# Half A's first layer norm: its transposes move from the GLA's PSUM bank to the three banks of the dense products

## The chip, the cores and the metric

One core of one Trainium2 chip runs one program. The metric is the device time of one execution in microseconds (us), the median of several runs; lower is better. Before the change it is 3109.51 us, the median of three runs that lie between 3102.37 and 3113.97 us.

## The reference

The program is one inference step of a two-layer streaming encoder on 1024 prompt frames of a new stream and 64 frames of a running stream, all in float32, width 1024. Layer 0 projects its input and feeds two token mixers, RWKV-7 (eight heads of 64, a matrix state that is carried from chunk to chunk) and GLA (chunked linear attention, four heads, state 64 by 128, also carried). Their outputs are joined and go through an output projection. Layer 1 has softmax attention over the frame's own chunk of 64 and the eight chunks before it. In each layer the mixer's result is added to the scaled input and normalised, then a SwiGLU of hidden width 2816 follows, with a second norm:

```
x = layer_norm(DEEPNORM_ALPHA * x + mix, ln1_w, ln1_b)
x = layer_norm(DEEPNORM_ALPHA * x + swiglu(x, ffn_w_in, ffn_w_out), ln2_w, ln2_b)
layer_norm(x) = (x - mean) * rsqrt(var + 1e-5) * w + b
```

The outputs are the frames after layer 1, the mixers' states and the attention's keys and values.

## The kernel before, in words

**Halves.** The 1088 frames lie in two halves. Half A has 448 columns: 384 prompt frames and the 64 frames of the running stream, so four token tiles of 128, 128, 128 and 64. Half B has the other 640 prompt frames. Half B's mixers need half A's states, but half A's dense work does not need half B's mixers, so the two are put beside each other.

**Products.** Every dense product is made in three passes with operands split into a high and a low part (`hi`, `lo`): high times high, high times low, low times high. `gemm_ws` (L116) holds 128 weight columns and streams the half's activations, all columns of a half at once; `gemm_ts` (L128) holds a tile of tokens and streams 512 weight columns. The 64 frames of the running stream have a packed form: their high and low parts lie side by side and two passes do, after which VectorE adds both halves of the result (L827 and L829).

**PSUM.** There are eight banks at this stage. Three, tag `g` of the pool `gp`, are handed out by `bank()` (L140) and take every dense product. Five belong to the mixers (`sbank`, L403): tags `a` (one bank), `b` (one), `c` (two) for RWKV-7 and `d` (one) for GLA, where the GLA's scores and transposed keys (`gpa`), outputs and state updates (`gps`) and transposed output (`gpy`) take turns. `sbank` gives the `d` bank to any name that is not in its table:

```
STAGE = {"pa": "a", "pb": "a", "pt": "a", "pz": "b", "ps": "c", "py": "c", "pss": "c", "gpa": "d", "gps": "d", "gpy": "d"}
tag = self.STAGE.get(name, "d")
self.tpsum = lambda: self.sbank("tps")
```

`tpsum` is what the layer norm (L899), the cache set-up (L1132) and the key part of `qk` (L1173) call for a bank to transpose into. So with the third line, which `run` sets at L1350, the layer norm's transposes use the GLA's one bank.

**The place.** `run` starts half B's mixers as two generators, `r` (RWKV-7, 24 steps) and `g` (GLA, 20 steps, one chunk of one head pair each), writes four steps of each (`self.PRE`), then half A's output projection with its layer norm (L1399), then the remaining steps of both, then half A's SwiGLU (`ffn`, L1405). In `proj` (L856) the second group of weights has the layer norm as its `after`: in `tsg` (L841 to L846) each token tile gets its two products of 512 columns, each added to the accumulator by VectorE, and then `tile(i)` of the layer norm.

**One tile of the layer norm** (L877 to L909): two `bn_stats` (L884) and an aggregate (L886) on VectorE, the reciprocal root on GpSimd (L888, L889), then for each half of 512 columns, j = 0 and 1, the scaling (VectorE L892; for j = 0 then ScalarE L894 and GpSimd L895, for j = 1 VectorE L897). Then `tpsum()` gives a bank, TensorE transposes four blocks of 128 columns into it (L902), and `split` (L111) empties it: ScalarE writes the high part into `xh` (L113) and VectorE the low part into `xl` (L114). After that the bank can be given to another tile. Four token tiles with two halves make eight such uses of a bank.

The SwiGLU's first product streams all 448 columns, so its passes over the column blocks 0 to 3 wait for j = 0 of all four tiles, and those over 4 to 7 for j = 1.

**The order of the work.** A planner orders the instructions of each engine when the program is built (`schedule_with_timeline_sim=True`, L1611). It goes by its own model of times, prefers what was written earlier in the program, and gives a tile its PSUM bank when the first instruction that writes it is put in the order. On the chip each engine then keeps that order, and an instruction that waits holds up all that stand behind it on its engine. VectorE, ScalarE and GpSimd are shared by the layer norm, the products' evacuation, the splitting of weights (L101, L106, L108) and the mixers.

Of the kernel before, what the change touches and what calls it, by code (L numbers as in the profile page):

```python
# [83 lines left out]
class Kern:  # L84
# [1255 lines left out]
    def run(self):  # L1340
# [55 lines left out]
        for _ in range(self.PRE):  # L1396
            next(r)
            next(g)
        self.proj(0, acc0, "w_om", self.layer_norm(0, acc0, "ln1", 0), pa)  # L1399
        for _ in r:  # L1400
            next(g, None)
        for _ in g:
# [212 lines left out]
```

## Time and profile before

| | us |
|---|---|
| median of three runs | 3109.51 |
| their lowest and highest | 3102.37, 3113.97 |
| the profiled execution's own time | 3102.95 |
| its span, first to last instruction | 3101.2 |
| TensorE busy in the span | 3007.5 |
| VectorE busy | 2016.0 |
| GpSimd busy | 1366.7 |
| ScalarE busy | 1270.8 |

PE is TensorE's matmul, PEld its weight load, DVE VectorE, ACT ScalarE, POOL GpSimd, SPq the queue that issues the transfers. A timeline's row gives the start and the duration in us, the engine, the line of the kernel, the operation, the tiles as output<-inputs, shapes and the number of instructions; in brackets stands the idle time before it and who ended it. A row of the table by stretches gives for each engine its busy time and number of instructions, then the clock that TensorE was granted (1.00 is full), the transfers' share and rate. Matmuls overlap, so the durations of neighbours add up to more than the time between their starts. Between 606.9 and 641 us after the span's start there is no dense product but the first of the SwiGLU; I call this stretch the gap.

### The profile page before, as it was taken

The page shows a single profiled execution, that of the slowest core. Times are in us where ns is not written, and L with a number is a line of the kernel's source. Part 1 is how long each engine was busy: PE and PEld are TensorE (multiplying, and loading weights), DVE is VectorE, ACT ScalarE, POOL GpSimd, SP SyncE. Part 2 cuts the span into 40 slices and gives each one's busy share as a digit, 9 for nine tenths or more (in the row PEclk, how much of TensorE's full clock was granted, in tenths as well). Part 3 has the DMA queues.
Part 4 walks back from the last instruction along what each step waited for, and adds up shares of the span by engine and source line. Part 5 has one row for each costly group of instructions (what it writes and reads, how often), then busy time and mean ns, then how long its engine had stood idle before and what let it go on. Part 6 is the DMA issues. An engine that isn't in the chain of part 4 may idle for free.

```text
span 3101.2 us, 50069 instructions
## 1 busy us (share of the span) xinstructions
PE 3007.5 (97%) x17468; PEld 2676.5 (86%) x17468; DVE 2016.0 (65%) x4941; ACT 1270.8 (41%) x2761; POOL 1366.7 (44%) x1489
## 2 busy tenths in 40 slices
PE   8999999899999999999999999999999999899998
PEld 7888888688888888798999898898899988899987
DVE  5677875879898764455554466245566668866667
ACT  4454554344454334243443132355444434333322
POOL 2354534444454334343342233244445546654444
PEclk9999999889999999999999999999899999999999
DMA  6553334533533228343342222866454443322212
GB/s 195 148 161 115 109 110 124 146 104 106 151 105 106 91 97 294 118 153 120 113 134 98 82 95 101 247 200 175 121 153 135 117 175 122 122 86 80 98 68 75
DMA packets 298492, 399.29 MB, mean 129 GB/s; under 512 B 125504, under 2 KB 218552, under 8 KB 298240
## 3 DMA queue, kind: packets, MB, share of 16 engines
q1 hardware_dynamic: 297088, 393.48, 41.2%
q8 instruction: 138, 2.26, 0.3%
q10 hardware_dynamic: 1152, 2.62, 0.2%
q14 instruction: 114, 0.93, 0.1%
HBM read 323.63 MB, written 75.51 MB: 129 GB/s over the span
## 4 chain that ended last, share of the span: by engine, by line
PE 77%; DVE 8%; DMA 7%; POOL 2%; issue 2%; ACT 2%; SPq 1%; POOLq 0%; ACTq 0%; DVEq 0%
PE gps L124 11%; PE gps L126 11%; PE gps L125 11%; PE gps L135 7%; PE gps L136 7%; PE gps L138 7%; PE gps L1065 3%; PE gps L1066 3%; PE gps L1067 3%; PE op L1328 2%; PE tp L1302 2%; DVE t L549 1%; DVE x L551 1%; PE sps L1286 1%; PE sps L1287 1%
## 5 line engine op out<-in xcount | busy, mean ns | idle before, releaser
L108 POOL TENSOR_TENSOR wl<-wr,wh 128x512 fp32r<-128x512 f32 (+2 forms) x297 | 521.7, 1760 | 669.3 <-ACT wh L101 612.0
L124 PE MATMUL gps<-xh,wh 128*128 128x320 f32 (+1 forms) x2188 | 747.7, 342 | 12.5 <-ACT xh L215 6.0
L125 PE MATMUL gps<-xl,wh 128*128 128x320 f32 (+1 forms) x2188 | 746.5, 341 | 0.6 <-DVE xl L216 0.6
L126 PE MATMUL gps<-xh,wl 128*128 128x320 f32 (+1 forms) x2188 | 745.9, 341 | 0.3 <-DVE wl L106 0.2
L101 ACT CAST wh<-wr 128x1024 fp32r<-128x1024 f32 x360 | 375.6, 1048 | 465.9 <-PE gps L125 135.6
L106 DVE TENSOR_TENSOR wl<-wr,wh 128x512 fp32r<-128x512 f32 (+2 forms) x297 | 293.8, 990 | 242.2 <-ACT wh L101 239.8
L124 PEld LDWEIGHTS gps<-xh,wh 128*128 128x128 f32 x2188 | 415.6, 190 | 34.4 <-ACT xh L215 6.0
L126 PEld LDWEIGHTS gps<-xh,wl 128*128 128x128 f32 x2188 | 415.6, 190 | 18.6 <-issue 0.8
L125 PEld LDWEIGHTS gps<-xl,wh 128*128 128x128 f32 x2188 | 415.5, 190 | 18.3 <-DVE xl L216 1.0
L1297 POOL TENSOR_SCALAR s<-s,mx 128x640 f32<-128x640 f32 (+5 forms) x144 | 205.3, 1426 | 258.7 <-DVE mx L1296 236.3
L138 PE MATMUL gps<-wh,xl 128*128 128x512 f32 x661 | 258.9, 397 | 5.4 <-DVE xl L216 4.8
L135 PE MATMUL gps<-wh,xh 128*128 128x512 f32 x661 | 259.9, 399 | 3.9 <-DVE acc L829 1.9
L136 PE MATMUL gps<-wl,xh 128*128 128x512 f32 x661 | 261.5, 397 | 0.0
L135 PE MATMUL gps<-wh,hh 128*128 128x512 f32 x572 | 224.8, 396 | 1.6 <-ACT wh L101 1.3
L136 PE MATMUL gps<-wl,hh 128*128 128x512 f32 x572 | 225.5, 396 | 0.0
L827 DVE TENSOR_TENSOR acc<-acc,gps 128x512 f32<-128x512 f32 x216 | 143.6, 680 | 89.6 <-PE gps L138 82.3
L138 PE MATMUL gps<-wh,hl 128*128 128x512 f32 x484 | 189.6, 397 | 1.6 <-DVE hl L943 1.6
L549 DVE TENSOR_TENSOR t<-lt,x 16x48 f32<-16x48 f32 (+9 forms) x540 | 149.3, 276 | 36.0 <-DMA lt<-l_d 25.5
L1295 ACT ACTIVATE s<-s,mx 128x640 f32<-128x640 f32 (+5 forms) x144 | 96.4, 669 | 149.6 <-DVE mx L1294 145.2
L138 PEld LDWEIGHTS gps<-wh,xl 128*128 128x128 f32 x661 | 124.9, 189 | 33.8 <-DVE xl L216 5.4
L135 PEld LDWEIGHTS gps<-wh,xh 128*128 128x128 f32 x661 | 125.0, 190 | 32.8 <-issue 2.5
L136 PEld LDWEIGHTS gps<-wl,xh 128*128 128x128 f32 x661 | 125.2, 189 | 28.0 <-DVE wl L106 1.1
(406 smaller groups left out, 6312.0 us busy)
## 6 DMA issues: line engine op xcount, KB each, us to landing
wr<-in_w_fi SPq DMA_DIRECT2D x176, 512.0 KB
wr<-in_w_fo SPq DMA_DIRECT2D x88, 512.0 KB
wr<-in_w_in SPq DMA_DIRECT2D x44, 512.0 KB
wr<-in_w_qk SPq DMA_DIRECT2D x32, 512.0 KB
wr<-in_w_o SPq DMA_DIRECT2D x24, 512.0 KB
qs<-qd SPq DMA_DIRECT2D x32, 320.0 KB
wr<-in_w_om SPq DMA_DIRECT2D x16, 512.0 KB
wr<-in_w_v SPq DMA_DIRECT2D x16, 512.0 KB
```

Of the source, the lines that this page charges most:

```text
L101: self.A.copy(hi, raw)
L106: self.V.tensor_tensor(lo[:, :h], raw[:, :h], hi[:, :h].bitcast(F32), op=ALU.subtract)
L108: self.G.tensor_tensor(lo[:, h:], raw[:, h:], hi[:, h:].bitcast(F32), op=ALU.subtract)
L124: self.T.matmul(ps, hi[:, kt, :], xh, start=(kt == 0), stop=False)
L125: self.T.matmul(ps, hi[:, kt, :], xl, start=False, stop=False)
L126: self.T.matmul(ps, lo[:, kt, :], xh, start=False, stop=(kt == nk - 1))
L135: self.T.matmul(ps, xh, wh, start=(i == 0), stop=False)
L136: self.T.matmul(ps, xh, wl, start=False, stop=(lo is None and i == n - 1))
L138: self.T.matmul(ps, cols(lo(kt)), wh, start=False, stop=(i == n - 1))
L549: V.tensor_tensor(tv, lt[:, j, w:16].unsqueeze(2).to_broadcast([m, r, w]), x[:, 0, j, 0:w].unsqueeze(1).to_broadcast([m, r, w]), op=ALU.mult)
L827: self.V.tensor_tensor(a, a, ps[:m], op=ALU.add)
L1297: G.tensor_scalar(s[:m, :nk], s[:m, :nk], mx[:m, 3:4], None, op0=ALU.mult)
```

## The change

Around half A's output projection in layer 0, `tpsum` is set to `bank` and set back afterwards:

```
-        self.proj(0, acc0, "w_om", self.layer_norm(0, acc0, "ln1", 0), pa)
+        self.tpsum = self.bank
+        self.proj(0, acc0, "w_om", self.layer_norm(0, acc0, "ln1", 0), pa)
+        self.tpsum = lambda: self.sbank("tps")
```

The eight tiles of transposes of this one layer norm are then taken from the three `g` banks, which they share with the products, and no longer from the `d` bank, which is left to the GLA. `bank()` counts its calls and, once a second pool of banks exists (from L1493 on), picks the pool by the count modulo 8. The change adds eight calls, so the choice at every later call is the same. No instruction is added or taken out: 32 transposes, eight ScalarE casts and eight VectorE subtractions get another address. What uses `tpsum` later (the cache set-up beside the SwiGLU, half A's second norm and the rest) is as before. Since a bank is a resource of the planner, the order of all engines is planned anew from there on.

## The prediction

> **What bounds the kernel now.** I read the page's head first, then the table by stretches, then TensorE's and VectorE's timelines across the gap.
>
> ```profile
> span 3101.2 us, 50069 instructions
> ```
>
> ```profile
> 482.00:606.90 124.90, 110.19 (x670) 95.45 (x670) 82.00 (x235) 49.79 (x139) 51.92 (x80) 0.93 0.51 137
> 606.90:641.00 34.10, 28.16 (x136) 22.25 (x135) 29.78 (x77) 15.57 (x45) 22.86 (x30) 0.54 0.33 117
> 641.00:1152.00 511.00, 508.45 (x3076) 436.43 (x3076) 414.08 (x1268) 218.77 (x614) 223.64 (x341) 0.99 0.36 108
> 1152.00:1360.00 208.00, 199.33 (x944) 169.03 (x943) 107.49 (x163) 74.41 (x104) 90.14 (x67) 0.98 0.60 199
> 1900.00:2200.00 300.00, 286.95 (x1706) 262.49 (x1706) 147.03 (x339) 134.45 (x264) 126.07 (x108) 0.97 0.64 191
> 2600.00:3101.00 501.00, 476.45 (x2732) 439.94 (x2730) 348.44 (x470) 172.77 (x245) 267.74 (x213) 0.98 0.26 91
> ```
>
> TensorE sets the time nearly everywhere: of the 511 us of half A's SwiGLU it is idle 2.55. The gap, 606.9 to 641, is the exception that the change touches: the granted clock is 0.54, VectorE works 29.78 of 34.10 us, and the SwiGLU waits for the layer norm. So the change can win two things: a shorter gap, and GLA work moved from the SwiGLU's stretch, where each us of TensorE counts, into the gap.
>
> Seven of the eight uses of the layer norm's one bank on TensorE (L902), with two instructions near its end, and on VectorE what empties the bank (L114) and what comes before it; the rows between are left out:
>
> ```profile
> 599.40 0.60 PE L902 MATMUL tps<-ident,acc 128*128 128x128 f32 x4
> 605.50 0.63 PE L902 MATMUL tps<-ident,acc 128*128 128x128 f32 x4
> 616.79 1.11 PE L902 MATMUL tps<-ident,acc 128*128 128x128 f32 x4
> 621.22 1.08 PE L902 MATMUL tps<-ident,acc 128*128 128x128 f32 x4 [0.44 <-DVE xl L114]
> 625.26 1.09 PE L902 MATMUL tps<-ident,acc 128*128 128x128 f32 x4 [0.65 <-DVE xl L114]
> 633.50 0.69 PE L902 MATMUL tps<-ident,acc 64*128 64x64 f32 x4
> 636.14 0.37 PE L618 MATMUL ps<-uv,tok 128*64 128x64 f32 x1
> 639.98 0.69 PE L902 MATMUL tps<-ident,acc 64*128 64x64 f32 x4
> 640.59 0.74 PE L125 MATMUL gps<-xl,wh 128*128 128x448 f32 x1
> ```
>
> ```profile
> 602.25 0.74 DVE L897 SCALAR_TENSOR_TENSOR acc<-acc,rstd,gb 128x512 f32<-128x512 f32 x1
> 604.68 0.67 DVE L114 TENSOR_TENSOR xl<-tps,xh 128x512 fp32r<-128x512 f32 x1
> 607.69 2.31 DVE L549 TENSOR_TENSOR t<-lt,x 16x28 f32<-16x28 f32 x1
> 613.62 0.66 DVE L827 TENSOR_TENSOR acc<-acc,gps 64x512 f32<-64x512 f32 x1
> 614.21 0.67 DVE L114 TENSOR_TENSOR xl<-tps,xh 128x512 fp32r<-128x512 f32 x1
> 617.53 0.69 DVE L829 TENSOR_TENSOR acc<-acc,gps 64x512 f32<-64x512 f32 x1
> 620.39 0.68 DVE L114 TENSOR_TENSOR xl<-tps,xh 128x512 fp32r<-128x512 f32 x1
> 624.42 0.69 DVE L114 TENSOR_TENSOR xl<-tps,xh 128x512 fp32r<-128x512 f32 x1
> 629.91 0.74 DVE L897 SCALAR_TENSOR_TENSOR acc<-acc,rstd,gb 64x512 f32<-64x512 f32 x1 [0.33 <-POOL rstd L889]
> 635.33 0.41 DVE L114 TENSOR_TENSOR xl<-tps,xh 128x256 fp32r<-128x256 f32 x1
> 641.16 0.39 DVE L114 TENSOR_TENSOR xl<-tps,xh 128x256 fp32r<-128x256 f32 x1
> ```
>
> Three of the seven handovers are tight: the split ends at 605.35, 621.07 and 625.11, and the next transposes start 0.15 us later. Tile 1's second half was scaled by 602.99 and was transposed only at 621.22. The last tile's second half was scaled at 630.65, its bank was empty at 635.74, and its transposes came at 639.98, behind RWKV-7 work that the planner had put there.
>
> **The change, part by part.** No instruction comes or goes, so the instructions themselves cost nothing. Three things can move the time.
>
> *First, the last handover.* With a bank of its own the last half can follow the other one: the transposes at 633.50 end where the next instruction starts, about 634.1, and 0.6 us more brings the second set to 634.7. Then the SwiGLU's L125 hangs on the split at 635.33, which ends at 635.74, and could start at about 635.8 where it starts at 640.59: 4.8 us earlier. What ran in the meantime, 636.14 to 639.98 (3.84 us, at a clock of 0.54), has to be done later, at full clock, for about half, 1.9 us. The net is -2.9 us.
>
> *Second, the handovers before it.* Tiles 1 and 2 can be transposed and split as soon as they are scaled. The splits cost VectorE the same 0.67 us each, whenever they come. What can be won is that no layer norm work is left waiting when the last tile's sums arrive. The trace has a stage without a shared bank: half A's second norm, whose eight uses go round other mixer banks.
>
> ```profile
> 1165.44 0.69 DVE L829 TENSOR_TENSOR acc<-acc,gps 64x512 f32<-64x512 f32 x1
> ...
> 1176.36 0.41 DVE L114 TENSOR_TENSOR xl<-ps,xh 128x256 fp32r<-128x256 f32 x1
> ```
>
> From the last sum to the end of the last split it takes 11.3 us (1165.44 to 1176.77); in the gap it takes 24.0 (617.53 to 641.55). The difference, 12.7 us, is the most that the first two parts can win together. In these 12.7 us TensorE is busy for 28.16/34.10 of the time, 10.5 us, at half clock, so some 5.2 us return later: -7.5 net. The other end is zero, if VectorE's order and not the bank sets the gap. I take -5.0, between -2.9 and -7.5, because three tight handovers say that the bank counts beyond the last one, and because VectorE, 87% busy, keeps the rest.
>
> *Third, the GLA.* Its rows on TensorE around the gap, with the product that follows each piece, and two groups of its instructions in the SwiGLU's stretch:
>
> ```profile
> 591.88 0.28 PE L756 MATMUL gpy<-ident,gon 128*128 128x128 f32 x1
> 647.38 0.33 PE L725 MATMUL gpa<-gqk,gbqk 128*128 128x64 f32 x2
> 647.58 0.45 PE L125 MATMUL gps<-xl,wh 128*128 128x448 f32 x1
> 652.23 0.38 PE L738 MATMUL gps<-gv,gba 128*128 128x128 f32 x2
> 652.82 0.45 PE L124 MATMUL gps<-xh,wh 128*128 128x448 f32 x1
> ```
>
> ```profile
> L409 DVE TENSOR_TENSOR gbqk<-gqk,bdk 128x256 f32<-128x256 f32 x15 | 6.8, 456 | 0.3 <-PE gps L739 0.2
> L742 POOL TENSOR_SCALAR gse<-gS,geb 128x128 f32<-128x128 f32 x15 | 12.1, 805 | 12.8 <-DVE gS L744 10.6 <-DVE x L551 2.1
> ```
>
> It has no TensorE work from 591.88 to 647.38, when the layer norm leaves the bank. Its next step can go on in the gap now. Its steps follow each other at some 20 us (this one and the next start at 647.38 and 666.07), so one or two fit there. Between the starts, a step costs the SwiGLU's stretch 0.2 us for the scores (647.38 to 647.58), 0.59 for the outputs (652.23 to 652.82) and about 0.1 for the last transpose: 0.9. Two steps save 1.8 us there. On VectorE a step has six instructions, the longest 456 ns, so at most 2.7 us; two steps put up to 5.4 us in front of, or between, the layer norm's, where VectorE is the busiest engine. The planner prefers what is written earlier, which is the layer norm, so most of it should fall into waits. The ends are -1.8 and +3.6; I take 0.
>
> What the GLA brings along on GpSimd can also slow VectorE, as a weight split does in the gap now:
>
> ```profile
> 606.41 3.55 POOL L108 TENSOR_TENSOR wl<-wr,wh 128x1024 fp32r<-128x1024 f32 x1 [2.28 <-ACT wh L101]
> ```
>
> Beside it L549, at 607.69, takes 2.31 us for 28 elements. The Trainium skill (SBUF — State Buffer, section "Who interferes with whom") says that a VectorE instruction with two inputs in SBUF contends with a GpSimd instruction that reads SBUF, and that the one issued first holds the shared port; this trace agrees (2.31 us). By this rule a GLA step's scaling of the state (L742, 805 ns) could hold VectorE once a step, 1.6 us for two, and the sum would be 3106.1 where it is 3104.5 without.
>
> **The sum.** 3102.95 (the profiled execution's own time, span 3101.2 and 1.75 around it) less 5.0 is 3097.95. That execution lies 6.56 us below the median of the runs, so against the median I predict 3109.5 - 5.0 = **3104.5 us**. About 0.5%, 15.5 us, is what a measurement of this kernel can tell from no change; my forecast lies within it.
>
> **The rivals.**
>
> *The bank was not the limit.* VectorE sets the gap; splits come no earlier because VectorE's order is the same. For it: 29.78 of 34.10 us busy, and TensorE's waits for the bank add up to only 1.09 us (0.44 and 0.65). Against it: the last handover, where VectorE had nothing to do with the 4.2 us. Time: 3109.5.
>
> *The products' banks run short: slower.* The last tile's two packed products and the tiles 0 and 1 of the layer norm, written before them and so preferred, want the same three banks. If tiles 0 and 1 hold all three, the last packed product starts late. Its eight matmuls end at 606.6 now, and its sum is taken at 613.62.
>
> ```profile
> 606.19 0.39 PE L136 MATMUL gps<-wl,xpk 128*128 128x512 f32 x1
> ```
>
> Nothing is lost as long as it ends by 613.6. If its bank comes only with the split at 614.21, which ends at 614.88, eight matmuls of 0.4 at half clock bring it to 618, and the last tile is 4.4 us late: 3113.9. It decides once a layer norm half holds a product's bank past about 611 with the other two taken as well. Against it: two banks come free at 604.75 and 605.35 in the order of now.
>
> *The new plan is luckier or worse elsewhere.* The plan is made anew from here on, with a model that isn't the chip. From 1152 on TensorE's idle time is 8.67 + 13.05 + 24.55 = 46.3 us in three stretches (length less busy). A third to a half of it is 15 to 23 us: 3081 to 3089 where it is saved on top of the gain of 5, 3120 to 3133 where it is added, with and without that gain. For it: nothing in this trace shows how much a plan moves. Against it: the stretches with idle time begin with transfers and norms that stay as they are.
>
> *The tight end.* Everything goes as in the second norm and two GLA steps fit in: -7.5 - 1.8 = -9.3, so 3100.
>
> *The change doesn't do what it says.* If the planner still puts the last half's transposes behind RWKV-7's work at 639.98, the bank is there and unused. The time is that of the first rival.
>
> **How the numbers follow.** My forecast, 3100 to 3108: 0.38. The bank was not the limit, or the plan leaves it unused: 0.18. Banks run short: 0.12. The tight end: 0.10. A new plan that is luckier by a third to a half of the idle time: 0.13; worse: 0.09. Faster by over 0.5% (below 3094) is the luckier plan, and 0.03 of the tight end with a little of the same luck: 0.16. Slower by over 0.5% (above 3125) is two thirds of the worse plan, 0.06, and 0.04 of the short banks with some of it: 0.10. Within: 0.74. The range reaches into both plans, from 3085 to 3123; the runs before alone spread over 11.6 us.
>
> **What the changed profile would show.** L902 writes `gps` tiles in the gap. Right: the last half's transposes follow the other half's within 1 us, the distance from the last sum (L829) to the last split (L114) falls from 24.0 to between 11 and 19 us, and the gap is about 5 us shorter; `gpa` and `gpy` appear between 592 and 641, and in the SwiGLU's stretch TensorE still idles below 5 us. The first rival: L829 to L114 stays near 24. Short banks: TensorE waits before L135 or L136 on `xpk`, and the sum at 613.62 comes later than about 618. A new plan: the gap changes as I say, but the stretches after 1152 differ from the rows above by more than 5 us. I am wrong if the gap grows, or if the total moves by more than 15 us while the gap does not.

## The result, and the profile after

The changed kernel is slower: 3122.01 us, the median of five runs between 3116.84 and 3126.81, against 3105.07 us for the kernel before on the same chip. The ratio is 1.0052, with a 95% interval of [1.0038, 1.0065]: 16 us lost, where the prediction had 5 won. All ratios below are to the kernel before in the same comparison. Its medians lay between 3101.6 and 3105.1 in these, all below the 3109.51 that were given at first.

The profiled span grew by 19.0 us, from 3101.2. TensorE's timeline across the gap, the rows where one kind of work gives way to the next; the columns are those of the prediction's timelines:

```profile
span 3120.2 us, 50083 instructions
```

```profile
600.52 1.09 PE L902 MATMUL gps<-ident,acc 128*128 128x128 f32 x8
601.38 0.48 PE L135 MATMUL gps<-wh,xh 128*128 128x512 f32 x1
...
608.06 0.39 PE L138 MATMUL gps<-wh,xl 128*128 128x512 f32 x1
609.49 0.43 PE L725 MATMUL gpa<-gqk,gbqk 128*128 128x64 f32 x2 [0.54 <-DVE gy L758]
615.84 1.97 PE L902 MATMUL gps<-ident,acc 128*128 128x128 f32 x8 [2.13 <-POOL acc L895]
617.46 0.77 PE L135 MATMUL gps<-wh,xh 128*128 128x512 f32 x1
...
624.64 0.39 PE L138 MATMUL gps<-wh,xl 128*128 128x512 f32 x1
635.24 1.97 PE L902 MATMUL gps<-ident,acc 128*128 128x128 f32 x8
636.86 0.78 PE L135 MATMUL gps<-wh,xpk 128*128 128x512 f32 x1
...
641.61 0.39 PE L136 MATMUL gps<-wl,xpk 128*128 128x512 f32 x1
643.91 0.39 PE L725 MATMUL gpa<-gqk,gbqk 128*128 128x64 f32 x2
656.81 1.19 PE L902 MATMUL gps<-ident,acc 64*128 64x64 f32 x8
661.00 0.74 PE L125 MATMUL gps<-xl,wh 128*128 128x448 f32 x1
1171.82 0.60 PE L902 MATMUL pz<-ident,acc 128*128 128x128 f32 x4
```

Read down the line numbers: eight transposes, a tile's products, eight transposes, the next tile's products, and so on. Products and transposes of the layer norm strictly alternate. Before, the last product began at 606.19, with two of the eight sets of transposes done, and the other six followed. Now tile 1's products begin 0.86 us after tile 0's transposes begin, tile 2's 1.62 us after tile 1's, and the packed ones of tile 3 1.62 us after tile 2's. From the end of its products each tile needs 7.4, 10.2 and 14.8 us until its own transposes (608.45 to 615.84, 625.03 to 635.24, 642.00 to 656.81). These stretches used to overlap with other tiles' products; now they stand in a row.

The kernel before starts its second norm here:

```profile
1152.16 0.60 PE L902 MATMUL pz<-ident,acc 128*128 128x128 f32 x4
```

The SwiGLU's first L125 comes at 661.00, 20.4 us later than before. From there to the second norm's first transposes it is 510.82 us (before 511.57, from 640.59 to 1152.16), and the rest of the span takes 1948.4 (before 1949.0). So the whole loss arises in the gap. The table by stretches, for two stretches of the length of the SwiGLU's, the second row of the kernel before:

```profile
659.90:1171.80 511.90, 506.46 (x3009) 431.85 (x3009) 399.62 (x1211) 209.41 (x578) 207.53 (x318) 0.99 0.36 106
```

```profile
640.60:1152.20 511.60, 509.05 (x3078) 436.94 (x3078) 414.68 (x1270) 219.27 (x614) 223.86 (x342) 0.99 0.36 108
```

TensorE has 2.6 us less to do there, since GLA steps have moved ahead of it (L725 at 609.49, 625.34 and 643.91), but it idles 5.4 us instead of 2.6. What GLA gave was not kept.

### The profile page after: what moved, and what is told of

The parts are those of the page before. It is cut to its first block, busy times and chain, and to the rows that moved or that the text cites. A ratio compares the mean times of both kernels' runs of the same rounds, so it can differ in the third digit from the quotient of the medians.

```text
span 3120.2 us, 50083 instructions
## 1 busy us (share of the span) xinstructions
PE 3009.3 (96%) x17468; PEld 2673.5 (86%) x17468; DVE 2019.6 (65%) x4941; ACT 1269.2 (41%) x2761; POOL 1352.7 (43%) x1489
## 4 chain that ended last, share of the span: by engine, by line
PE 78%; DVE 8%; DMA 7%; POOL 2%; issue 2%; ACT 2%; SPq 1%; POOLq 0%; ACTq 0%; DVEq 0%
PE gps L124 11%; PE gps L125 11%; PE gps L126 11%; PE gps L135 8%; PE gps L136 8%; PE gps L138 7%; PE gps L1065 3%; PE gps L1067 3%; PE gps L1066 3%; PE op L1328 2%; PE tp L1302 2%; DVE t L549 1%; DMA wr<-in_w_in 1%; PE sps L1286 1%; DVE x L551 1%
## 5 line engine op out<-in xcount | busy, mean ns | idle before, releaser
L125 PE MATMUL gps<-xl,wh 128*128 128x320 f32 (+1 forms) x2188 | 744.5, 340 | 0.6 <-DVE xl L216 0.6
L125 PEld LDWEIGHTS gps<-xl,wh 128*128 128x128 f32 x2188 | 413.9, 189 | 18.8 <-DVE xl L216 1.0
L138 PE MATMUL gps<-wh,xl 128*128 128x512 f32 x661 | 259.4, 398 | 5.4 <-DVE xl L216 4.8
L135 PE MATMUL gps<-wh,xh 128*128 128x512 f32 x661 | 260.7, 400 | 4.0 <-DVE acc L829 1.9
L136 PE MATMUL gps<-wl,xh 128*128 128x512 f32 x661 | 261.7, 397 | 0.0
L135 PE MATMUL gps<-wh,hh 128*128 128x512 f32 x572 | 225.5, 398 | 1.3 <-ACT wh L101 1.0
L136 PE MATMUL gps<-wl,hh 128*128 128x512 f32 x572 | 226.3, 398 | 0.0
L827 DVE TENSOR_TENSOR acc<-acc,gps 128x512 f32<-128x512 f32 x216 | 143.5, 679 | 95.5 <-PE gps L138 88.5
L138 PE MATMUL gps<-wh,hl 128*128 128x512 f32 x484 | 189.1, 396 | 0.0
L549 DVE TENSOR_TENSOR t<-lt,x 16x48 f32<-16x48 f32 (+9 forms) x540 | 140.2, 260 | 42.4 <-DMA lt<-l_d 32.2
L551 DVE TENSOR_TENSOR x<-x,t 16x48 f32<-16x48 f32 (+9 forms) x540 | 153.9, 285 | 10.4
L138 PEld LDWEIGHTS gps<-wh,xl 128*128 128x128 f32 x661 | 125.1, 189 | 33.7 <-DVE xl L216 5.3
L135 PEld LDWEIGHTS gps<-wh,xh 128*128 128x128 f32 x661 | 125.3, 190 | 32.7 <-issue 2.3
```

The lines of the kernel that those rows point to most:

```text
L125: self.T.matmul(ps, hi[:, kt, :], xl, start=False, stop=False)
L135: self.T.matmul(ps, xh, wh, start=(i == 0), stop=False)
L136: self.T.matmul(ps, xh, wl, start=False, stop=(lo is None and i == n - 1))
L138: self.T.matmul(ps, cols(lo(kt)), wh, start=False, stop=(i == n - 1))
L549: V.tensor_tensor(tv, lt[:, j, w:16].unsqueeze(2).to_broadcast([m, r, w]), x[:, 0, j, 0:w].unsqueeze(1).to_broadcast([m, r, w]), op=ALU.mult)
L551: V.tensor_tensor(x[:, 0, w:16, 0:w], x[:, 0, w:16, 0:w], tv, op=ALU.add)
```

## The experiments

Three theories. **A, the order:** tiles of one tag get their banks in the order in which the program writes them. The transposes of tile k are written ahead of the products of tile k+1, so with one tag for both these products can't overtake them, as they did before. That makes three links: products of tile 1 behind the norm of tile 0, of tile 2 behind that of tile 1, the packed ones behind that of tile 2. **B, the number:** three banks are too few for products and norm together. **C, the GLA:** its steps, let into the gap, take VectorE and GpSimd from the layer norm.

The runs are compared in time from a common point. Up to tile 0's first sum in the second group of weights (L827, in x1_order L829), VectorE's instructions stand in the same order in every run. Even so, single executions reach this sum at different times; here it is in the kernel before, then in the run x9_only2:

```profile
585.82 0.67 DVE L827 TENSOR_TENSOR acc<-acc,gps 128x512 f32<-128x512 f32 x1
```

```profile
590.53 0.67 DVE L827 TENSOR_TENSOR acc<-acc,gps 128x512 f32<-128x512 f32 x1
```

These 4.7 us arise ahead of the change: two executions of one kernel, x2 and x12, lie 6.9 us apart at this sum. The distance from it to the SwiGLU's first L125 is steadier, 52.8 us in both of these and 51.9 in both x4 and x11. It is the table's last column; in the kernel before it is 54.8, and the changed kernel's loss in the gap is 20.3 by it.

| run | what stands in the products' banks; order | median us | ratio, 95% interval | first sum to SwiGLU, us |
|---|---|---|---|---|
| changed kernel | all eight transposes | 3122.01 | 1.0052 [1.0038, 1.0065] | 75.0 |
| x1_order | none; products held behind norms by an added order | 3117.99 | 1.0045 [1.0032, 1.0057] | 82.3 |
| x5_first1 | tile 0 | 3113.84 | 1.0037 [1.0023, 1.0050] | 60.6 |
| x9_only2 | tile 2 | 3113.86 | 1.0034 [1.0022, 1.0045] | 58.1 |
| x10_first3 | tiles 0 to 2 | 3135.66 | 1.0101 [1.0087, 1.0114] | 76.8 |
| x3_last | tile 3 | 3103.28 | 1.0002 [0.9993, 1.0011] | 50.5 |
| x4_rwkvbank, x11_rwkvbank2 | none; RWKV-7's two banks | 3098.84, 3098.55 | 0.9985 [0.9976, 0.9994], 0.9991 [0.9981, 1.0001] | 51.9, 51.9 |
| x8_rotate | none; mixers' banks in turn | 3102.61 | 1.0010 [1.0000, 1.0019] | 53.0 |
| x2_prodfirst, x12_prodfirst2 | all eight; products written first | 3099.70, 3097.48 | 0.9986 [0.9974, 0.9997], both times | 52.8, 52.8 |
| x6_prodfirst_own | none; products written first | 3107.54 | 1.0013 [1.0004, 1.0022] | 58.5 |
| x7_prodfirst_ps | none; products first, RWKV-7's banks | 3102.46 | 0.9999 [0.9989, 1.0009] | 52.3 |

In four of these runs the edit does a second thing. The kernel picks the pool of every product from L1493 on by the number of `bank()` calls modulo 8. The change adds eight calls and leaves these choices alone, but x3, x5 and x9 add two and x10 adds six. So their totals hold another choice of pools in the last stages too, and what a link costs is better read from the last column.

### The order alone, with the bank of before

```
-                for nh in range(2):
-                    part(ws[nh], nh, i, t0, m)
+                with self.tc.issue_after(self.last_tp) if self.order_after and i else ExitStack():
+                    for nh in range(2):
+                        part(ws[nh], nh, i, t0, m)
```

`last_tp` is the last transpose of the tile before, set in the layer norm, and the order holds for this one projection. The transposes write the GLA's bank as before.

> The layer norm transposes into the GLA's bank as in the kernel before, and one ordering edge is added: on TensorE the products of token tile 1, 2 and 3 stand behind the transposes of the tile before, as they do in the changed kernel. No bank is shared with the products and the GLA stays shut out of its bank. Theory A (the order: tiles of one tag get their bank in the order of the program, so each tile's products stand behind the transposes of the tile before): about as slow as the changed kernel, 15 to 20 us above the kernel before, 3120 to 3126 us. Rival B (three banks are too few, the products wait for a bank to come free): no change, within 5 us of 3105. Rival C (the GLA, let into the gap, takes VectorE and GpSimd from the layer norm): no change, within 5 us of 3105.

It lost nearly as much, a ratio of 1.0045. The added lines move the line numbers: L905 is the transposes, L137 and L138 the packed products, L727 the GLA's scores. TensorE's timeline across the gap:

```profile
643.01 1.12 PE L905 MATMUL tps<-ident,acc 128*128 128x128 f32 x4 [0.57 <-DVE xl L116]
643.78 0.78 PE L137 MATMUL gps<-wh,xpk 128*128 128x512 f32 x1
...
670.90 0.74 PE L127 MATMUL gps<-xl,wh 128*128 128x448 f32 x1
675.88 0.33 PE L727 MATMUL gpa<-gqk,gbqk 128*128 128x64 f32 x2
```

The products' banks hold no transposes here, so B has no part in it; no GLA score comes in the gap, so C has none either. The order of products and norms alone is enough for a loss of this size. It is not made up of the same parts as in the changed kernel: the SwiGLU starts 27.5 us late by the last column, and 12.8 us come back in its stretch (498.7 us against 511.6), where TensorE is busy 11.6 us less (497.4 against 509.0), since more of RWKV-7's work was done in the longer gap: 12 of its state sums (L625 in the kernel before) stand between the first sum and the SwiGLU, against 8.

### The products written first, with the changed banks

```
+        done = []
+        norm = self.layer_norm(0, acc0, "ln1", 0)
+        self.proj(0, acc0, "w_om", done.append, pa)
+        self.tpsum = self.bank
+        for i in done:
+            norm(i)
```

> The transposes go into the products' three banks as in the changed kernel, but the program writes the products of all four token tiles first and then the four tiles of the layer norm. Theory A: the slowdown goes, 3097 to 3107 us, since no product is written behind a transpose. Rival B: only partly better, since the eight uses and the eight products still share three banks and the GLA's bank stays unused by them: 3110 to 3120. Rival C: as slow as the changed kernel, 3115 to 3125, because the GLA has its bank.

This keeps the three banks and all eight uses of them, and only the order of writing is another. It is 0.14% faster than the kernel before, and was so again in a second comparison:

> The same kernel as in the run with the products written first and the norms in the products' banks, a second time, for the same reason. Nothing is left out. If the gain is of the kernel: 0.9974 to 0.9997 again. If it was the chance of one comparison: an interval around 1.

TensorE's timeline of the first of the two runs:

```profile
607.40 0.40 PE L136 MATMUL gps<-wl,xpk 128*128 128x512 f32 x1
609.95 0.66 PE L902 MATMUL gps<-ident,acc 128*128 128x128 f32 x4
610.88 0.33 PE L725 MATMUL gpa<-gqk,gbqk 128*128 128x64 f32 x2
...
634.64 0.69 PE L725 MATMUL gpa<-gqk,gbqk 128*128 128x64 f32 x2
...
642.98 0.57 PE L125 MATMUL gps<-xl,wh 128*128 128x448 f32 x1
```

The last product starts at 607.40, near the 606.19 of before, and now every set of transposes stands behind it. The same three banks and eight uses do no harm in this order, and neither does GLA in the gap at 610.88 and 634.64 (C falls). The cost of writing the products first shows too: the first transposes wait until 609.95.

Here the products are done before the norm takes a bank, so this run doesn't try the banks with both in them at once. For that the changed kernel's own trace decides. Its tile 2 has its second sum here, on VectorE:

```profile
625.07 0.69 DVE L827 TENSOR_TENSOR acc<-acc,gps 128x512 f32<-128x512 f32 x1
```

From 625.76, when it ends, until tile 2's transposes at 635.24 nothing stands in any of the three banks, and still the packed products, which need no norm, start only at 636.86. Between tile 1's second sum, which ends at 609.18, and its transposes at 615.84 it is the same. A lack of free banks can't hold products back where all three are free (B falls).

### One link, the first

```
+        def after(i):
+            self.tpsum = self.bank if i == 0 else lambda: self.sbank("tps")
+            norm(i)
```

> Only tile 0's two norm transposes take the products' banks; tiles 1 to 3 use the GLA's bank as before. Nothing is left out. A (banks of one tag go in program order, so the products behind the transposes wait for them) leaves one link of the three: tile 1's products start behind tile 0's transposes, at about 601, and with tile 2's and the packed ones (some 20 us of them) end near 621 instead of 606; from there the packed tile needs its norm, 17 to 24 us, so the SwiGLU starts at 640 to 647, 0 to +7 us, and the whole takes 3102 to 3110. The third link (last products behind tile 2's norm) is gone, and with it most of the 19 us. If instead each use of the products' banks by a norm cost the same (two of the eight uses here), the loss would be a quarter of it, +4.8 us, with the products ending by 611.

```profile
600.08 1.86 PE L902 MATMUL gps<-ident,acc 128*128 128x128 f32 x8
601.69 0.48 PE L135 MATMUL gps<-wh,xh 128*128 128x512 f32 x1
...
619.38 0.39 PE L136 MATMUL gps<-wl,xpk 128*128 128x512 f32 x1
...
645.95 0.74 PE L125 MATMUL gps<-xl,wh 128*128 128x448 f32 x1
...
1160.36 0.60 PE L902 MATMUL pz<-ident,acc 128*128 128x128 f32 x4
```

The order is as A has it: tile 1's products stand behind tile 0's transposes, and the last product starts at 619.38, near the 621 forecast. The SwiGLU starts 5.4 us later than before, 5.8 by the last column, within the 0 to 7. The whole lost more than A had forecast: 0.37% is 11.5 us. The profiled span is 10.9 longer; past the gap the SwiGLU's stretch is about 2.8 longer, and what comes after it as much. There two executions of one kernel, x2 and x12, differ by 3.7 us, so this last part may be chance.

### One link, the third

The same edit with `i == 2`: the case that the rival of the short banks had in mind, the packed product alone late.

> Only tile 2's two norm transposes take the products' banks; tiles 0, 1 and 3 use the GLA's bank as before. Nothing is left out. It is the third link alone, the one that the rival of short banks priced at 4.4 us at most: the last, packed product stands behind tile 2's norm. A: the packed products start only after tile 2's transposes, which in the kernel before came at 617 to 622, and end 6 us later at the gap's low clock, 624 to 628 instead of 606.6; from there the packed tile's norm takes the 15 to 17 us that it took in the changed kernel, so the SwiGLU starts at 640 to 645, 0 to +5 us, 3102 to 3109. If the price of 4.4 us had been right for a bank that is merely held, the packed products would end by 611 and the whole would not be measurably slower.

```profile
619.88 1.92 PE L902 MATMUL gps<-ident,acc 128*128 128x128 f32 x8
621.45 0.78 PE L135 MATMUL gps<-wh,xpk 128*128 128x512 f32 x1
...
626.77 0.39 PE L136 MATMUL gps<-wl,xpk 128*128 128x512 f32 x1
...
648.60 0.74 PE L125 MATMUL gps<-xl,wh 128*128 128x448 f32 x1
...
1163.83 0.60 PE L902 MATMUL pz<-ident,acc 128*128 128x128 f32 x4
```

The packed products stand behind tile 2's transposes, as A says, 621.45 to 627.2 (forecast 624 to 628 for their end). The SwiGLU starts at 648.60, which looks 8.0 us late; but 4.7 of these stand ahead of the change. By the last column it is 3.3 us late, within A's 0 to 5 and no more than the rival's 4.4. Where the time went before that differs from the forecast: without the 4.7 us the packed products end at 622.4, earlier than forecast, and from there to the SwiGLU it is 21.4 us, not 15 to 17. The loss of the whole, 0.34% or 10.5 us, is above the forecast 5 and above the rival's 4.4 (the interval begins at 0.22%, 6.8 us). Of it 3.3 us stand in the gap and 3.7 in the SwiGLU's stretch (515.2 us against 511.6); the rest lies behind it or in the spread of single executions. Place and price in the gap were right, the price of the whole too low.

### Three links, without the last tile

```
+            self.tpsum = self.bank if i < 3 else lambda: self.sbank("tps")
```

> Tiles 0 to 2 take the products' banks for their norm transposes, tile 3 the GLA's bank as before. Nothing is left out. All three links stand, without the change at tile 3 that was tried alone. A: nearly the whole of the loss, the last packed products at 636 to 642 and the SwiGLU's first product at 655 to 665, 3115 to 3124. If tile 3's use of the products' banks were part of the loss, it would be smaller by that part: below 3113.

It lost 1.01%, 31 us: more than the changed kernel, and more than any theory said. Its gap, on TensorE:

```profile
637.26 0.48 PE L135 MATMUL gps<-wh,xpk 128*128 128x512 f32 x1
...
664.15 0.74 PE L125 MATMUL gps<-xl,wh 128*128 128x448 f32 x1
```

The packed products and the SwiGLU come as A says, the SwiGLU 23.6 us later than before, 22.0 by the last column. The first and the third link alone cost 5.8 and 3.3 there; the second alone was not run, so how the three add up stays open. The rest of the loss arises in the last SwiGLU, far from the edit. Here is L1065, the first pass of its first product, with the times of its first and last matmul; first of the kernel before, then of this run:

```profile
L1065 PE MATMUL gps<-xh,wh x344: 303/309/632, 2657.7 to 3060.8; 128*128 128x320 f32 x172
...
L1065 PE MATMUL gps<-xh,xh x8: 306/390/636, 2650.1 to 2656.9; 128*128 128x320 f32 x8
```

```profile
L1065 PE MATMUL gps<-xh,wh x344: 303/309/597, 2678.1 to 3095.4; 128*128 128x320 f32 x172
...
L1065 PE MATMUL gps<-xh,xh x8: 306/310/337, 2673.7 to 2692.3; 128*128 128x320 f32 x8
```

From the first to the last of them it is 410.7 us before and 421.7 here; in all the other runs it is between 410.7 and 414.9. So of the span's 34.6 us more, 23.6 are there when the SwiGLU of layer 0 starts and 11.0 arise in that last stage. The products there take their pools by a count that is six calls ahead, and the order differs: in the runs with no or eight calls more, VectorE's instructions stand in the order of the kernel before from 2546 us of its span at the latest, but here only from 2833 on, and in x3, x5 and x9 from 2797 on. That the other pools cost the 11.0 us is argued from this and was not run by itself.

### The last tile alone

```
+            self.tpsum = self.bank if i == 3 else lambda: self.sbank("tps")
```

> Only the last token tile (64 tokens, two uses) transposes into the products' banks; tiles 0 to 2 use the GLA's bank as before. Nothing is written behind the last tile in this projection. Theory A: no slowdown, and the part of the prediction on the last handover is tested alone: 3 to 5 us less than before, 3099 to 3103 us; the transposes of the last tile's two halves follow each other within 1 us. Rival B: no change or slightly slower, 3105 to 3110. Rival C: between, 3105 to 3112, since the GLA gets its bank for the last third of the gap.

VectorE and TensorE at the end of the gap, as two timelines:

```profile
619.78 0.69 DVE L829 TENSOR_TENSOR acc<-acc,gps 64x512 f32<-64x512 f32 x1
...
636.40 0.40 DVE L114 TENSOR_TENSOR xl<-gps,xh 128x256 fp32r<-128x256 f32 x1
```

```profile
601.70 0.60 PE L902 MATMUL tps<-ident,acc 128*128 128x128 f32 x4
...
634.71 1.11 PE L902 MATMUL gps<-ident,acc 64*128 64x64 f32 x8
...
638.62 0.74 PE L125 MATMUL gps<-xl,wh 128*128 128x448 f32 x1
...
1152.57 0.60 PE L902 MATMUL pz<-ident,acc 128*128 128x128 f32 x4
```

Nothing is written behind tile 3 in this projection, so there is no link, and what the prediction had said of the last handover holds: both halves are transposed together at 634.71, and from the last sum to the last split it is 17.0 us instead of 24.0. From the first transposes, which stand ahead of anything that the edit moves, to L125 it is 36.9 us, before 41.2: 4.3 us won. To the second norm 1.9 of them are left (550.9 us against 552.8). In the time as a whole nothing can be told: 1.0002, with an interval of -2.2 to +3.4 us.

### Other banks

For the norm's transposes, the tag of RWKV-7's two banks (`ps`):

```
+        self.tpsum = lambda: self.sbank("ps")
```

> All four token tiles transpose into RWKV-7's pair of banks (tag c), neither the products' nor the GLA's. Theory A: no slowdown, since the tag is not that of the products: 3098 to 3107 us, and the GLA has TensorE rows in the gap. Rival B: the same, 3098 to 3107. Rival C: slow, 3112 to 3125, because the GLA is let into the gap as in the changed kernel.

```profile
608.82 0.33 PE L725 MATMUL gpa<-gqk,gbqk 128*128 128x64 f32 x2
...
629.60 0.69 PE L725 MATMUL gpa<-gqk,gbqk 128*128 128x64 f32 x2 [0.78 <-DVE gy L758]
```

It frees the GLA's bank as the change does, and two GLA steps run in the gap, but it puts nothing between the products. It won 0.15%, which refutes C once more. A second comparison gave 0.09%, with an interval that just includes 1:

> The same kernel as in the run with RWKV-7's tag of banks for the norm's transposes, a second time, since 0.15% is little beside the spread of this kernel. Nothing is left out. If the gain is of the kernel: 0.9976 to 0.9994 of the time before again. If it was the chance of one comparison: an interval around 1.

Going round the mixers' tags as half A's second norm does (`("pa", "pz", "ps", "gpa", "ps")`, in turn) brought no gain:

> The norm's transposes go round four of the mixers' tags (as half A's second norm does), so that no two transposes in a row share a bank, and neither the products' banks nor the GLA's own bank for its sums is touched alone. Nothing is left out. A predicts no link between the products: they end by about 607, and the gap is that of the second norm's stretch at best: 3095 to 3103. If the norms' hold on banks of both mixers slows these: 3103 to 3110.

Products end as forecast, and so does the time, 3102.61, but the ratio 1.0010 lies at or just above no change.

### Products first, with other banks

> The bank of before, but all dense products of the projection are written ahead of the norm of its four tiles. Nothing is left out. It takes the products-first order alone, without freeing the GLA's bank, and says what gave the 0.14% of the run with both. If the order alone gave it: 3098 to 3101. If freeing the GLA's bank gave it (its steps go into the gap): no change, 3101 to 3105, and no GLA scores between 606 and 640.

The order of writing without the change of banks loses 0.13%, which neither case of the expectation had: it is no source of gain by itself. Its gap is 3.7 us longer by the last column.

> All dense products written ahead of the norms, and the norms' transposes in RWKV-7's tag of banks. Nothing is left out. It joins the two changes that were a little faster. If both gains come from the GLA's steps moved into the gap, they don't add: 3098 to 3101. If they add: 3094 to 3097. If RWKV-7's recurrence waits for its banks behind the norms' transposes: 3102 to 3108.

Products first and RWKV-7's banks together give 0.9999: the two small gains don't add, and the time, 3102.46, falls in the third case's range; whether RWKV-7's waits are the reason stays open. **Only the products written first with the change's banks have an interval below 1 in both comparisons: 0.9986 of the time before, 4.3 us (0.9 to 8.1). From the kernel with RWKV-7's banks this can't be told apart.**

## Why the prediction was wrong

The forecast, 3104.5 us and no measurable change, failed: a loss of over 0.5% had been given a chance of 0.10. The 3122.01 us lie within the range of 3085 to 3123, but its upper end was there for a worse plan of the later stages, which did not come; that is luck. By the prediction's own steps:

**The step that failed** is the rival *the products' banks run short*, and a sentence that the forecast and the rivals all rest on: that the planner gives a tile its bank when the first instruction that writes it is put in the order. By it a product written later may take a bank ahead of a norm written earlier, as soon as one is free. So the prediction looked for two free banks, found them at 604.75 and 605.35, and let only the last packed product be late, by 4.4 us. The runs show another rule; how the planner comes to it they don't show. In the changed kernel and in each run with a norm tile in the products' banks, the products written behind that tile's transposes start behind them, and they do not where the tags differ. It isn't the number of free banks: with an order added and the banks of before the loss is 1.0045, and with all eight uses in the three banks but the products written first there is a gain; and in the changed kernel all three stood empty for 9.5 us ahead of tile 2's transposes, with the packed products still behind these. Three links, not one late product, make the 20.3 us at the SwiGLU's start. For the one link that the rival named, its price of 4.4 us was about right there (x9: 3.3 us), though not for the whole (10.5 us, in a run that also changed the later pools); what it missed is the number of links.

**The last handover** was right as a mechanism: in x3 it is 4.3 us earlier where 4.8 were forecast, and 1.9 us net at the second norm where 2.9 were. In the changed kernel too the last two halves are transposed together. It is simply small beside the links.

**The handovers before it**: the second norm as a measure held for its distance. From the last sum to the end of the last split it is 15.0 us in the changed kernel (forecast 11 to 19), here on VectorE:

```profile
644.89 0.67 DVE L829 TENSOR_TENSOR acc<-acc,gps 64x512 f32<-64x512 f32 x1
...
659.47 0.42 DVE L114 TENSOR_TENSOR xl<-gps,xh 128x256 fp32r<-128x256 f32 x1
```

What failed is taking this distance for the gap's length. The last sum itself moved from 617.53 to 644.89, and a shorter way from there could not make up for it.

**The GLA** was taken at nothing, between -1.8 and +3.6. That holds for the whole: four steps, not two, begin between 592 us and the SwiGLU (one at 592.18 and the three shown), and the SwiGLU's stretch is 0.7 us shorter. Where GLA was freed without a link (x4, x11) the kernel was 0.09 to 0.15% faster and the SwiGLU's stretch 2.5 and 2.3 us shorter. But in x4 TensorE has as much to do in it as before (508.8 us against 509.0); what went is idle time, 0.2 us instead of 2.6, and not the moved work that the 1.8 were made of.

**The signs named beforehand** were half right. The gap grew, which the prediction had called the sign of being wrong, and the sum at 613.62 did come later than 618 (642.04). But no wait of TensorE before L135 or L136 on `xpk` appears. Between 608.4 and 661.0 us it was busy for most of the time, much of it with the mixers' work, which the planner had put there, and idled 14.0 us, 11.9 of them before the mixers' own instructions; only the 2.13 us at 615.84 stand before a norm's transposes. In the SwiGLU's stretch it idles 5.4 us, not below 5. So a loss that is made by an order shows little in the rows of waits. It shows when the orders of two kernels are laid side by side.

**A new plan elsewhere** did nothing in the changed kernel (the rest of the span is 0.6 us shorter) and so can't explain its loss. The 11 us of x10 stand in a stage whose pools were chosen by another count, so they are not a plan's luck alone. As one kernel's two executions, x2 and x12, differ by 3.7 us behind the second norm, differences of about 0.1% between kernels here say little of their edits.

## What to carry to other kernels

A bank's tag is not only room; under a planner that serves one tag in the order of writing, it is also an order. Before two producers are put on one tag, write down the order of their calls: if a late step of one (a norm that needs statistics) stands ahead of an early step of the other (a product that needs only weights), the early step can wait while banks stand empty, as here. Either keep the tags apart or write what is ready first ahead, and look for the effect in the order on TensorE before its waits. When runs of different edits are compared, count from an instruction that stands ahead of all of them, and see that the edit moves nothing else, such as a counter that later stages read.

## What was not expected of the hardware

In the changed kernel one of the two scalings of the last tile (L892) takes several times what the others of this layer norm take. The group of this line in the changed kernel, with the shortest, median and longest in ns and the first and last start, then of the kernel before, then GpSimd's timeline beside it in the changed kernel:

```profile
L892 DVE SCALAR_TENSOR_TENSOR acc<-acc,mv,gb x8: 714/746/3336, 593.6 to 650.3; 128x512 f32<-128x512 f32 x6, 64x512 f32<-64x512 f32 x2
```

```profile
L892 DVE SCALAR_TENSOR_TENSOR acc<-acc,mv,gb x8: 731/734/747, 594.3 to 626.6; 128x512 f32<-128x512 f32 x6, 64x512 f32<-64x512 f32 x2
```

```profile
650.73 2.34 POOL L108 TENSOR_TENSOR wl<-wr,wh 128x1024 fp32r<-128x1024 f32 x1
```

The longest is the last, which starts at 650.3; it takes 3.34 us instead of 0.73, and ends just after GpSimd's weight split (650.73 to 653.07). So 2.6 us of the last tile's way may come from a neighbour that the later place of the norm brought. Beside another such split, from 642.48 to 644.82, a sum of L829 (643.01), which reads one of its two inputs from PSUM, kept its 0.69 us. The Trainium skill (SBUF — State Buffer, section "Who interferes with whom") says that a VectorE instruction with two SBUF inputs contends with a GpSimd instruction that reads SBUF; the trace agrees, with the 3.34 us. No run took the split away, so the cause is argued and not shown.
